# An mLSTM layer's sigmoids placed behind all its exponentials, and longer planned landings for small transfers

## The chip, the cores and the metric

The kernel runs on one core of one Trainium2 chip. The metric is the device time of one execution in microseconds (us), the median of several runs. A core has a matrix engine (TensorE, PE in the profile; PEld is its weight load), a vector engine (VectorE, DVE), a scalar engine (ScalarE, ACT), a general engine (GpSimd, POOL) and a queue for transfers (SyncE, SP). Each engine works through its own list of instructions in order; the engines wait for each other by semaphores alone.

## The reference, cut to what matters

A trunk of two layers over 256 tokens of width 1024, in float32. Each layer is a half-step SwiGLU, a mixer and another SwiGLU, each followed by a layer norm of the scaled sum. The mixer of the first layer is a bidirectional mLSTM, that of the second a windowed attention. Cut to the lines the change touches:

```python
p = x @ w_in                               # q, k, v, the output gate o, and gates i, f of both directions
wts = jnp.exp(dmat - m_out[..., None])     # per head and direction, from the scanned gates
s_qk = jnp.einsum('bhcjd,bhcsd->bhcjs', q, k) * wts
num = jnp.einsum('bhcjs,bhcsv->bhcjv', s_qk, v) + ...
h = num / den[..., None]
h = (h - mu) * lax.rsqrt(var + LN_EPS)     # per head
out = jax.nn.sigmoid(o.astype(jnp.float32)) * h
return out.astype(x.dtype) @ w_out
```

So an mLSTM layer has two nonlinear functions on ACT after its gates: exponentials for the weights of four heads, and sigmoids for the output gate.

## The kernel before, in words

Every product is made in three passes over a high and a low part of both operands (`mm3`): ACT writes the high part (`w_hi`, `k_hi`, `a_hi`), DVE the rest (`w_lo`, `k_lo`, `a_lo`). The SwiGLU stages and the value projection use a seven-product scheme; POOL adds some of its weight sums by accumulating transfers.

In the mixer, `qk` (units named `q`) projects queries and keys of two heads at a time. The last unit of a pair evacuates `kT` and calls `weights(h)`: POOL broadcasts the row maxima `most` over the partitions (`partition_broadcast`), ACT makes six exponentials into `wt` from `ucol`, POOL masks the diagonal blocks (`affine_select`). `scores(h)` (H0 to H3) multiplies keys by queries on PE, then by `wt` on DVE, and splits into `a_hi` and `a_lo`. `mixed(h)` (M0 to M3) multiplies by the values, divides by `den` and normalises; POOL raises `hrs` to the power -0.5, and the next DVE steps wait for that. `gate_units` (units `u`) make the output gate on PE. The first half of it for both token blocks is done early and only copied to `sg`; `sigmoids` (named `sig`) later loads the sigmoid's table and turns these copies into sigmoids. `gate_out` multiplies `h` by `sg`.

`MIXES` lists these pieces in the order in which the program is recorded; it sets PE's order outright. The order on ACT, DVE, POOL and SP is worked out by a planner (`Book`). It gives each step a due time, counted back from its readers, and then places steps one after the other by readiness and due time, with a cost for each. Of a transfer from POOL it assumes that it lands `LANDING + LOADING` (3600 ns) after its issue, and in the due times likewise. These costs order the work; they do not run on the chip.

A table load (`preload_act_table`) is ordered behind the users of the table before it, and each exponential or sigmoid behind the load recorded last. In the order before, the sigmoid's load stands ahead of the exponentials of heads 2 and 3, and three of the loads among these, and one further on, are in no line of the kernel: the compiler puts a load where a function's table isn't the one last loaded.

The small tensors that POOL loads are `few` (gate weights, gate biases, norm gain, attention sinks; each its own transfer) and `most`.

Of the kernel before, what the change touches and what calls it, by code (L numbers as in the profile page):

```python
# [50 lines left out]
OWN = [(5, 0), (6, 0), (7, 0)]  # L51
MIXES = ('P1*2 u*4 P2*2 u*2 p u*2 x1 u*4 x3 g x2 u*4 x4 S1*2 S2*2 S4*2 S3*2 q*7 A22*2 q*1 c q*29 '
         'sig q*1 H0 q*2 H1 q*8 M0 q*16 u*2 H2 M1 u*1 H3 u*3 M2 u*2 M3 u*8')
FIRST = "P1*2 d T1 P2*2 S1*2 S2*2 d S3*2 S4*2 d A22*2 T0"
FULL = "P1*2 d T1 P2*2 S1*2 S2*2 d S3*2 S4*2 d A22*2 T0 d"
SHUT = "P1*2 d T1 P2*2 S1*2 S2*2 d*2 S3*2 S4*2 A22*2 T0"
# [3 lines left out]
ISSUE = 600.0  # L60
LANDING = 2200.0
LOADING = 1400.0
ADDING = 5500.0
QUEUED = 6000.0
RING = {"SP": (2000.0, 1250.0), "POOL": (2900.0, 1150.0)}
# [182 lines left out]
SILU, EXPS, SIGMOID = "silu", "exps", "sigmoid"  # L248
TABLE = {AF.Silu: SILU, AF.Exp: EXPS, AF.Ln: EXPS, AF.Sigmoid: SIGMOID}


class Book:
# [13 lines left out]
    def note(self, engine, name, args, kw):  # L266
        views = [x for x in [*args, *kw.values()] if isinstance(x, View)]
        outs = [args[0]] if args and isinstance(args[0], View) else []
        if "accum_out" in kw:
            outs.append(kw["accum_out"])  # L270
        if name == "tensor_tensor_reduce":
            outs.append(args[-1])
        ins = [v for v in views if not any(v is o for o in outs)]
        s = Step(len(self.steps), engine, name, args, kw, outs, ins)
        self.steps.append(s)
        for v in views:
            if v.room not in s.rooms:
                s.rooms.append(v.room)
        for r in s.rooms:
            if r.kind == "const":  # L280
                continue
            if r.first is None:
                r.onto = r.kind == "bank" and engine != "PE"
                r.first, r.nth = s.n, len(self.rooms[r.kind])
                self.rooms[r.kind].append(r)
            r.last = s.n
            r.left += 1
            r.steps.append(s)
        for v in ins:
            r, (q, i) = v.room, v.place()  # L290
            for p in q:
                s.deps.update(r.writer[p, i].tolist())
        for v in outs:
            r, (q, i) = v.room, v.place()
            inside = np.zeros(r.n, bool)
            inside[i] = True
            for p in q:
                s.deps.update(r.writer[p, i].tolist())
                s.deps.update(r.pe[p, i].tolist())
            kept = []  # L300
            for other, q_, i_ in r.readers:
                if other is s:
                    continue
                if set(q_) & set(q) and inside[i_].any():
                    s.deps.add(other.n)
                    if set(q_) <= set(q) and inside[i_].all():
                        continue
                kept.append((other, q_, i_))
            r.readers = kept
            for p in q:  # L310
                r.writer[p, i] = s.n
                r.pe[p, i] = -1
        for v in ins:
            r, (q, i) = v.room, v.place()
            if engine == "PE":
                for p in q:
                    r.pe[p, i] = s.n
            else:
                r.readers.append((s, q, i))
        if name.startswith("preload"):  # L320
            s.deps.update(self.table_users)
            self.loaded, self.table_users = s.n, [s.n]
        elif name == "activation" and args[2] in TABLE:
            s.deps.add(self.loaded)
            self.table_users.append(s.n)
        s.deps -= {-1, s.n}
        self.cost(s)
        return s
# [64 lines left out]
    def latest(self):  # L393
        steps = self.steps
        extra = [[] for _ in steps]
        for kind, rooms in self.rooms.items():
            held, free = [], HOMES[kind][1]
            for r in rooms:
                if free:
                    free -= 1  # L400
                else:
                    held.sort(key=lambda x: x.last)
                    old = held.pop(0)
                    assert old.last < r.first, ("no room", kind, r.name, [x.name for x in held])
                    for s in old.steps:
                        extra[s.n].append(r.first)
                held.append(r)
        t = 0.0
        for s in steps:
            if s.engine == "PE":  # L410
                s.due = t
                t += s.takes
        for s in reversed(steps):
            if s.engine == "PE":
                continue
            after = s.later + s.takes
            if s.name == "dma_start":
                after += ADDING + LANDING if s.kw.get("accum_op") is not None else LANDING + LOADING
            s.due = min([steps[d].due for d in [*s.succ, *extra[s.n]]], default=t + 5000.0) - after

    def sequence(self):
# [54 lines left out]
        while len(given) < len(steps):  # L476
            best = None
            for e, list_ in todo.items():
# [7 lines left out]
                for n in cands:  # L486
                    s = steps[n]
# [21 lines left out]
            s = steps[n]  # L509
# [7 lines left out]
            s.lands = s.end + s.later  # L517
            if s.name == "dma_start":
                if e == "POOL" and s.kw.get("accum_op") is None:
                    s.lands = s.end + LANDING + LOADING  # L520
                elif loads < len(RAMP):
                    dma = s.lands = RAMP[loads]
                    rings.t = dma - RING[e][1]
                    loads += 1
                else:
                    for n_, t_ in rings.add(s).items():
                        steps[n_].lands = t_ + SPARE[steps[n_].engine]
                        if steps[n_].engine == "SP":
                            dma = max(dma, t_) if n_ == n else dma
                    loads += 1  # L530
# [1097 lines left out]
```

## Time and profile before

| | |
|---|---|
| median of 3 runs | 916.67 us (916.41 to 917.3) |
| profiled execution | 916.12 us, span 914.4 us |
| busy: PE, DVE, ACT, POOL | 98%, 90%, 72%, 18% of the span |
| moved by DMA | 220.07 MB, mean 241 GB/s |
| table loads on ACT | 10, 12.8 us in all |

The span is from the first instruction to the last; the execution's time is 1.7 us longer. In timeline rows the columns are start and length in us, engine, line, operation, output and inputs by the program's names, shapes and count; brackets hold the idle time ahead of it and what ended it. "Issue" there means that nothing the profile shows was waited for. All recorded operations share one line of the source, so they are told apart by their tiles.

### The profile page before, as it was taken

The page shows a single profiled execution, that of the slowest core. Times are in us where ns is not written, and L with a number is a line of the kernel's source. Part 1 is how long each engine was busy: PE and PEld are TensorE (multiplying, and loading weights), DVE is VectorE, ACT ScalarE, POOL GpSimd, SP SyncE. Part 2 cuts the span into 40 slices and gives each one's busy share as a digit, 9 for nine tenths or more (in the row PEclk, how much of TensorE's full clock was granted, in tenths as well). Part 3 has the DMA queues.
Part 4 walks back from the last instruction along what each step waited for, and adds up shares of the span by engine and source line. Part 5 has one row for each costly group of instructions (what it writes and reads, how often), then busy time and mean ns, then how long its engine had stood idle before and what let it go on. Part 6 is the DMA issues. An engine that isn't in the chain of part 4 may idle for free.

```text
span 914.4 us, 12652 instructions
## 1 busy us (share of the span) xinstructions
PE 893.3 (98%) x4375; PEld 744.0 (81%) x4375; DVE 825.4 (90%) x1011; ACT 659.7 (72%) x927; POOL 163.6 (18%) x200
## 2 busy tenths in 40 slices
PE   9999999999879999999999999999999999999996
PEld 7888888888867888888888888888898788888785
DVE  7999998799677999999889999997789999999974
ACT  6777676686856887776768867776689888677651
POOL 0121221220311211121011211130132231112100
PEclk9999999999999999999999999999999999999999
DMA  9999998937367889999985899999532778999931
GB/s 317 379 306 268 272 322 263 285 78 228 121 211 223 212 229 324 259 279 310 322 254 131 233 316 299 263 265 365 197 117 80 213 173 232 319 262 275 293 88 46
DMA packets 107744, 220.07 MB, mean 241 GB/s; under 512 B 7288, under 2 KB 23696, under 8 KB 107680
## 3 DMA queue, kind: packets, MB, share of 16 engines
q1 hardware_dynamic: 84000, 174.09, 53.9%
q0 software_dynamic: 23680, 45.18, 28.7%
q8 instruction: 34, 0.56, 0.2%
q14 instruction: 30, 0.25, 0.1%
HBM read 218.18 MB, written 1.05 MB: 240 GB/s over the span
## 4 chain that ended last, share of the span: by engine, by line
PE 71%; DVE 14%; issue 7%; ACT 4%; DMA 3%; POOL 1%; DVEq 0%; POOLq 0%; ACTq 0%
PE pw L597 44%; PE py L597 26%; DVE w_lo L597 7%; DMA b<-in_ffn_w_in_dram 2%; DVE b L597 1%; DMA raw<-in_ffn_w_out_dram 1%; ACT sc L597 1%; DVE e L597 1%; ACT L597 1%; ACT wt L597 1%; ACT w_hi L597 1%; DVE x L597 1%; DVE pr L597 0%; DVE h L597 0%; DVE pv L597 0%
## 5 line engine op out<-in xcount | busy, mean ns | idle before, releaser
L597 ACT CAST w_hi<-b 128x1024 fp32r<-128x1024 f32 x280 | 291.8, 1053 | 104.4 <-PE py L597 48.3
L597 DVE TENSOR_TENSOR w_lo<-b,w_hi 128x1024 fp32r<-128x1024 f32 x280 | 334.4, 1219 | 10.5 <-ACT w_hi L597 10.0
L597 PE MATMUL pw<-w_hi,S 128*128 128x512 f32 x640 | 205.8, 391 | 0.2 <-DVE h_lo L597 0.2
L597 DVE TENSOR_TENSOR w_lo<-raw,w_hi 128x1024 fp32r<-128x1024 f32 (+1 forms) x150 | 178.8, 1208 | 10.9 <-ACT w_hi L597 9.9
L597 POOL DMA_DIRECT2D b<-in_ffn_w_in_dram x80 | 96.9, 1214 | 502.8 <-DVE b L597 201.4
L597 ACT CAST w_hi<-raw 128x1024 fp32r<-128x1024 f32 (+1 forms) x150 | 155.1, 1041 | 36.0 <-PE pw L597 15.6
L597 PE MATMUL pw<-w_hi,xT_hi 128*128 128x512 f32 (+1 forms) x400 | 157.2, 395 | 1.4 <-DVE h_lo L597 1.0
L597 PE MATMUL pw<-w_hi,xT_lo 128*128 128x512 f32 (+1 forms) x400 | 154.8, 389 | 0.0
L597 PE MATMUL pw<-w_lo,xT_hi 128*128 128x512 f32 (+1 forms) x400 | 153.4, 386 | 0.0
L597 PEld LDWEIGHTS pw<-w_hi,S 128*128 128x128 f32 x640 | 120.1, 188 | 26.6 <-DVE h_lo L597 1.6
L597 PE MATMUL py<-w_hi,h_hi 128*128 128x512 f32 x317 | 125.5, 396 | 0.0
L597 PE MATMUL pw<-w_lo,S 128*128 128x512 f32 x320 | 124.5, 389 | 0.0
L597 PE MATMUL py<-w_hi,h_lo 128*128 128x512 f32 x317 | 123.7, 390 | 0.0
L597 PE MATMUL py<-w_lo,h_hi 128*128 128x512 f32 x317 | 123.4, 389 | 0.0
L597 DVE TENSOR_TENSOR b<-b,b 128x1024 f32<-128x1024 f32 x74 | 90.2, 1221 | 0.8
L597 PEld LDWEIGHTS pw<-w_hi,xT_lo 128*128 128x128 f32 x400 | 75.3, 188 | 17.5 <-DVE xT_lo L597 2.1
L597 PEld LDWEIGHTS pw<-w_hi,xT_hi 128*128 128x128 f32 x400 | 75.3, 189 | 17.2 <-DVE h_lo L597 1.8
L597 PEld LDWEIGHTS pw<-w_lo,xT_hi 128*128 128x128 f32 x400 | 75.1, 188 | 13.9
L597 PEld LDWEIGHTS pw<-w_lo,S 128*128 128x128 f32 x320 | 60.1, 188 | 12.2
L597 PEld LDWEIGHTS py<-w_hi,h_lo 128*128 128x128 f32 x317 | 59.5, 188 | 12.7
L597 PEld LDWEIGHTS py<-w_lo,h_hi 128*128 128x128 f32 x317 | 59.6, 188 | 11.8
L597 PEld LDWEIGHTS py<-w_hi,h_hi 128*128 128x128 f32 x317 | 59.5, 188 | 11.6
(208 smaller groups left out, 1134.7 us busy)
## 6 DMA issues: line engine op xcount, KB each, us to landing
b<-in_ffn_w_in_dram SPq DMA_DIRECT2D x152, 512.0 KB, 8.1
raw<-in_ffn_w_out_dram SPq DMA_DIRECT2D x88, 512.0 KB, 8.3
b<-in_ffn_w_in_dram POOLq DMA_DIRECT2D x80, 512.0 KB, 9.0
raw<-in_ffn_w_in_dram SPq DMA_DIRECT2D x36, 256.0 KB, 6.2
raw<-in_ml_w_in_dram SPq DMA_DIRECT2D x16, 512.0 KB, 6.5
raw<-in_at_w_in_dram SPq DMA_DIRECT2D x12, 512.0 KB, 9.0
b<-in_ml_w_in_dram SPq DMA_DIRECT2D x8, 512.0 KB, 6.7
raw<-in_ml_w_out_dram SPq DMA_DIRECT2D x8, 512.0 KB, 3.8
```

The costliest lines, as they stand in the source:

```text
L597: getattr(engines[s.engine], s.name)(*[real(x) for x in s.args], **{k: real(x) for k, x in s.kw.items()})
```

## The change

In `MIXES` the piece `sig` moves from ahead of H0 to behind the last `q` unit, that is, behind the exponentials of all four heads. The planner now notes which table is loaded and asserts that each function finds its own. And for plain transfers by POOL it assumes 6600 ns to land into `most` and 9500 ns into `few`, in the due times and in the placing.

```diff
-         'sig q*1 H0 q*2 H1 q*8 M0 q*16 u*2 H2 M1 u*1 H3 u*3 M2 u*2 M3 u*8')
+         'q*1 H0 q*2 H1 q*8 M0 q*16 sig u*2 H2 M1 u*1 H3 u*3 M2 u*2 M3 u*8')
...
+FEW = {"most": 6600.0, "few": 9500.0}
...
+            self.table = EXPS if name == "preload_act_table_set" else TABLE[args[0]]
         elif name == "activation" and args[2] in TABLE:
+            assert self.table == TABLE[args[2]], args[2]
...
-                after += ADDING + LANDING if s.kw.get("accum_op") is not None else LANDING + LOADING
+                after += ADDING + LANDING if s.kw.get("accum_op") is not None else FEW[s.outs[0].room.name] if s.engine == "POOL" else LANDING + LOADING
...
-                    s.lands = s.end + LANDING + LOADING
+                    s.lands = s.end + FEW[s.outs[0].room.name]
```

The order on PE and on SP stays the same, instruction by instruction. On the other engines it differs at a few places; three matter to the prediction. (The new file is three lines longer, so its rows read L600 where the old ones read L597.)

The first is ACT where the first pair's keys are evacuated (`k_hi`), ahead of H0. Before:

```order
L597 CAST q_hi<-pw 128x512
L597 ACTIVATE wt<-wt,ucol 128x128 x9
L597 CAST v_hi<-e_1978 128x2x256
L597 CAST w_hi<-raw 128x1024
L597 ACTIVATE k_hi<-pw 128x512
L597 ACTIVATE w_hi<-raw,few 128x1024 x2
L597 ACTIVATE wt<-wt,ucol 128x128 x3
L597 CAST a_hi<-wt 128x768
L597 ACT_TABLE_LOAD x2
L597 ACTIVATE wt<-wt,ucol 128x128 x6
```

And now:

```order
L600 CAST q_hi<-pw 128x512
L600 CAST v_hi<-e_1978 128x2x256
L600 CAST w_hi<-raw 128x1024
L600 ACTIVATE w_hi<-raw,few 128x1024
L600 ACTIVATE wt<-wt,ucol 128x128
L600 ACTIVATE k_hi<-pw 128x512
L600 ACTIVATE wt<-wt,ucol 128x128 x11
L600 ACTIVATE w_hi<-raw,few 128x1024
L600 CAST a_hi<-wt 128x768
L600 ACTIVATE wt<-wt,ucol 128x128 x6
```

`k_hi` has moved from behind nine exponentials and two casts to behind one exponential, and two loads of a table are gone. DVE at the same place, from the first `k_lo` to the first `a_lo`, before:

```order
L597 SCALAR_TENSOR_TENSOR k_lo<-pw,k_hi 128x512
L597 TENSOR_TENSOR w_lo<-raw,w_hi 128x1024
L597 TENSOR_TENSOR wt<-pw,wt 128x2x256
L597 TENSOR_TENSOR wt<-pw,wt 128x2x128
L597 TENSOR_TENSOR w_lo<-raw,w_hi 128x1024
L597 TENSOR_TENSOR a_lo<-wt,a_hi 128x768
```

And now:

```order
L600 SCALAR_TENSOR_TENSOR k_lo<-pw,k_hi 128x512
L600 TENSOR_TENSOR w_lo<-raw,w_hi 128x1024 x2
L600 TENSOR_TENSOR wt<-pw,wt 128x2x128
L600 TENSOR_TENSOR v_lo<-e_1978,v_hi 128x2x256
L600 TENSOR_TENSOR wt<-pw,wt 128x2x128
L600 TENSOR_TENSOR wt<-pw,wt 128x2x256
L600 TENSOR_TENSOR v_lo<-e_1949,v_hi 128x2x256
L600 TENSOR_TENSOR a_lo<-wt,a_hi 128x768
```

The products by `wt` stand behind one more weight difference and a `v_lo`, and a product of head 1 has come between those of head 0.

The second place is ACT from the first M0 to the second pair's `k_hi`, ahead of H2 (`den` and `h` belong to the mixes). Before:

```order
L597 ACTIVATE w_hi<-raw,few 128x1024
L597 CAST a_hi<-wt 128x768
L597 ACTIVATE den<-py 128x1
L597 ACTIVATE w_hi<-raw,few 128x1024
L597 ACTIVATE sg<-sg 128x512
L597 ACT_TABLE_LOAD
L597 ACTIVATE wt<-wt,ucol 128x128 x3
L597 ACTIVATE h_2419<-py,den 128x256
L597 ACTIVATE h_2425<-py,den 128x256
L597 ACTIVATE wt<-wt,ucol 128x128 x3
L597 ACTIVATE k_hi<-pw 128x512
```

And now:

```order
L600 ACTIVATE w_hi<-raw,few 128x1024
L600 CAST a_hi<-wt 128x768
L600 ACTIVATE h_2388<-py,den 128x256
L600 ACTIVATE h_2394<-py,den 128x256
L600 ACTIVATE w_hi<-raw,few 128x1024
L600 ACTIVATE wt<-wt,ucol 128x128
L600 ACTIVATE k_hi<-pw 128x512
L600 ACTIVATE wt<-wt,ucol 128x128 x5
L600 ACT_TABLE_LOAD
L600 ACTIVATE den<-py 128x1 x2
```

The sigmoids of the copies (`sg<-sg`) and the loads around them no longer stand ahead of `k_hi`; one load of the sigmoid's table follows the last exponential. Over the program ACT has six table loads where it had ten.

The third place is POOL in the same stage. The rows `ISA wt<-most` are the broadcasts, a bare `ISA` is a change of POOL's code. Before:

```order
L597 DMA most<-scan 4x256 x2
L597 ISA
L597 ISA wt<-most 128x256 x3
L597 AFFINE_SELECT wt<-wt 128x256 x2
L597 ISA wt<-most 128x256 x3
L597 AFFINE_SELECT wt<-wt 128x256 x4
L597 ISA wt<-most 128x256 x2
L597 AFFINE_SELECT wt<-wt 128x256 x2
L597 ISA
L597 TENSOR_TENSOR hrs<-hrs,few 128x2 x4
```

And now:

```order
L600 DMA most<-scan 4x256 x2
L600 ISA
L600 ISA wt<-most 128x256 x4
L600 AFFINE_SELECT wt<-wt 128x256 x2
L600 ISA wt<-most 128x256 x2
L600 AFFINE_SELECT wt<-wt 128x256 x4
L600 ISA wt<-most 128x256 x2
L600 ISA
L600 TENSOR_TENSOR hrs<-hrs,few 128x2
L600 AFFINE_SELECT wt<-wt 128x256 x2
L600 TENSOR_TENSOR hrs<-hrs,few 128x2 x3
```

The second change of code now stands right behind the last broadcast, and the masks of head 3 stand behind it and behind the first `hrs`. Further up, POOL issues the loads of the gate biases and gate weights one or two places earlier among its accumulating loads; the norm gain comes ahead of one `rs`, and the attention sinks ahead of one accumulating load.

## The prediction, made before the change was run

> **What bounds the kernel now.** I read the page first (span and busy time), then the waits of TensorE (PE), then the timeline of the one stage where PE waits.
>
> ```profile
> span 914.4 us, 12652 instructions
> PE 893.3 (98%) x4375; PEld 744.0 (81%) x4375; DVE 825.4 (90%) x1011; ACT 659.7 (72%) x927; POOL 163.6 (18%) x200
> ```
>
> PE is idle for 914.4 - 893.3 = 21.1 us in all. Half of that lies in 50 us of the mLSTM mixer, which is where the change works. The busy time of each engine there, and in its first three pieces of 5 us (columns: stretch, length, PE, weight load, DVE, ACT, POOL, granted PE clock, DMA share, GB/s):
>
> ```profile
> 230.00:280.00 50.00, 39.62 (x255) 35.44 (x254) 37.45 (x76) 38.91 (x80) 12.17 (x20) 0.97 0.58 195
> 230.00:235.00 5.00, 2.04 (x18) 1.83 (x16) 0.60 (x1) 3.94 (x11) 3.26 (x7) 1.00 0.30 105
> 235.00:240.00 5.00, 3.98 (x19) 3.78 (x20) 3.98 (x5) 4.78 (x9) 1.60 (x4) 0.66 0.01 3
> 240.00:245.00 5.00, 5.00 (x44) 5.00 (x43) 4.67 (x8) 4.98 (x12) 0.77 (x2) 1.00 0.58 206
> ```
>
> No engine fills the 50 us: PE works 39.6, DVE 37.5, ACT 38.9. They wait for each other in turn. What PE waits for between 225 and 284 us (us in total, times, longest):
>
> ```profile
> PE pw L597 <- ACT k_hi L597: 6.0, 2, 3.8
> PE py L597 <- ACT h L597: 1.6, 1, 1.6
> PE py L597 <- DVE h L597: 0.9, 1, 0.9
> PE py L597 <- DVE wt L597: 0.7, 1, 0.7
> PE py L597 <- DVE xT_lo L597: 0.6, 1, 0.6
> PE pw L597 <- DVE k_lo L597: 0.4, 2, 0.2
> ```
>
> These add up to 10.2 us. A further loss is the granted clock of 0.66 after the longest wait: from 235 to 240 us 19 matmuls take 3.98 us, while from 240 to 245 us 44 take 5.00, 0.114 each; 19 at that pace are 2.2, so 1.8 are lost. I count 1.5, as the restart itself is in it. **Ceiling: 10.2 + 1.5 = 11.7 us.** PE's order is the same throughout, so the change can move time only through what PE waits for.
>
> **Part 1, the first k_hi.** PE has run out of work at 232.04 and waits for the evacuation `k_hi` of the first two heads:
>
> ```profile
> 231.76 0.28 PE L597 MATMUL pw<-xT_hi,w_lo 128*128 128x256 f32 x1
> 235.79 0.38 PE L597 MATMUL pw<-q_hi,k_hi 128*128 128x256 f32 x1 [3.75 <-ACT k_hi L597]
> ```
>
> ACT at that time, and until the second `k_hi`:
>
> ```profile
> 231.06 2.74 ACT L597 ACTIVATE wt<-wt,ucol 128x128 f32<-128x128 f32 x9 [6.31 <-POOL wt L597]
> 233.70 0.60 ACT L597 CAST v_hi<-e 128x512 fp32r<-128x512 f32 x1
> 234.21 1.04 ACT L597 CAST w_hi<-raw 128x1024 fp32r<-128x1024 f32 x1
> 235.16 0.58 ACT L597 ACTIVATE k_hi<-pw 128x512 fp32r<-128x512 f32 x1
> 238.90 0.83 ACT L597 CAST a_hi<-wt 128x768 fp32r<-128x768 f32 x1 [0.21 <-DVE wt L597]
> 239.75 2.57 ACT L597 ACT_TABLE_LOAD   x2
> 244.80 1.28 ACT L597 ACT_TABLE_LOAD   x1
> 250.19 1.28 ACT L597 ACT_TABLE_LOAD   x1
> 253.97 0.58 ACT L597 ACTIVATE k_hi<-pw 128x512 fp32r<-128x512 f32 x1
> ```
>
> Before, nine exponentials, `v_hi` and a weight cast stand ahead of `k_hi`. In the new order one exponential does. That one still waits for POOL's first broadcast until 231.06 (nine take 2.74, so about 0.29 each); `k_hi` then runs from 231.35 to 231.93, before PE runs out. The casts now stand where ACT idled 6.31 us. The wait of 3.75 goes and with it the slow clock: 3.75 + 1.5 = **5.25 us**. DVE's `k_lo` (0.69) still follows `k_hi`, so its 0.2 stays here.
>
> **Part 2, what is late next: the first mix M0.** M0 needs `a_hi` and `a_lo` of head 0. The DVE rows that price its new order:
>
> ```profile
> 235.77 0.69 DVE L597 SCALAR_TENSOR_TENSOR k_lo<-pw,k_hi 128x512 fp32r<-128x512 f32 x1 [5.17 <-ACT k_hi L597]
> 236.38 1.22 DVE L597 TENSOR_TENSOR w_lo<-raw,w_hi 128x1024 fp32r<-128x1024 f32 x1
> 240.16 0.95 DVE L597 TENSOR_TENSOR a_lo<-wt,a_hi 128x768 fp32r<-128x768 f32 x1
> 241.03 0.41 DVE L597 TENSOR_TENSOR wt<-pw,wt 128x256 f32<-128x256 f32 x1
> 241.37 1.28 DVE L597 TENSOR_TENSOR v_lo<-e,v_hi 128x512 fp32r<-128x512 f32 x2
> 243.71 0.68 DVE L597 TENSOR_TENSOR wt<-pw,wt 128x512 f32<-128x512 f32 x1
> ```
>
> From the new `k_lo` end, 232.65: two `w_lo` 2.4, small product 0.35, `v_lo` 0.6, small product 0.35, large product 0.65 (each a little under its row, since neighbours overlap) give 237.0; ACT's `a_hi` 0.83 gives 237.85, `a_lo` 0.95 gives 238.8. PE comes from 232.04 with 42 matmuls (two scores of 6, ten projection units of 3) at 0.12 plus the 0.2, so at 237.3. It waits 0.55, and before the third product, which needs `a_lo`, 0.7 more. **Minus 1.25 us**; before, both operands were ready. Bounds: 0.3 if DVE runs its two weight differences during PE's own wait, 1.5 if one takes longer.
>
> **Part 3, the second k_hi.** ACT's time from 231.06 to 254.55 has almost no idle: 23.5 us of work stand ahead of and in the second `k_hi`. Out of that go four table loads, each of this price:
>
> ```profile
> L597 ACT ACT_TABLE_LOAD x10 | 12.8, 1283 | 0.9 <-PEq L1615 0.8
> ```
>
> 4 x 1.28 = 5.1; of ten loads six stay. The two sigmoids (1.2), `v_hi` and the weight cast (1.4 with overlap) and five exponentials (1.4) also leave this stretch. 23.5 - 9.1 = 14.4, plus some 0.9 of waiting for `a_hi`'s input: ACT could be through `k_hi` at 246.4. PE, 7.9 us of work after M0's effective start at 238.6, delivers the input at about 246.5 and has 1.4 us of gate units after it. So PE, not ACT, comes last: the second wait (6.0 - 3.75 = 2.25) and its `k_lo` (0.2) go. **2.45 us.** Here the loads are worth something; ACT idles again after 257 us, so their 5.1 us are not themselves a gain.
>
> **Part 4, the waits of the tail** (ACT h, DVE wt, DVE h, DVE xT_lo: 3.9 with roundings). They come from one event on POOL:
>
> ```profile
> 246.75 1.86 POOL L597 PARTITION_BROADCAST wt<-most  x2 [2.01 <-issue]
> 254.14 0.41 POOL L597 TENSOR_SCALAR_AFFINE_SELECT wt<-wt 128x256 f32<-128x256 f32 x1 [1.12 <-ACT wt L597]
> 261.66 0.73 POOL L597 TENSOR_TENSOR hrs<-hrs,few 128x2 f32<-128x2 f32 x1 [7.12 <-issue]
> 262.43 0.74 DVE L597 TENSOR_SCALAR h<-h,hmv,hrs 128x256 f32<-128x256 f32 x2 [2.88 <-POOL hrs L597]
> ```
>
> After the last mask (254.55) POOL issues nothing for 7.1 us: the order has an ISA row there, a reload of POOL's code. DVE waits 2.88 for `hrs` behind it, and everything on DVE afterwards is late. Now the reload stands right behind the last broadcast. That broadcast follows DVE's first scaled `w_lo` of the output weight, which comes 2.4 us after `a_lo`: 241.2 + 1.86 + 7.1 = 250.2, `hrs` done 250.95, against 262.40 before. PE is only 6.7 us ahead there (5.25 - 1.25 + 2.45 = 6.45, and roundings), so DVE's wait shrinks to about 1.3. Head 3's masks, now behind `hrs`, end at 251.75; DVE wants them about 254. I leave 1.3 of the 3.9 standing (0.3 at ACT h, 1.0 at the final transposes): **2.6 us**. Bounds 0 and 3.9.
>
> The Trainium skill (GPSIMD Engine Reference, 2.1 Instruction dispatch) puts the first call of freshly loaded POOL code at about 6 us (5.95 measured), invisible in the profile. The row here says 7.12, and the reload decides part 4: by the page `hrs` would be ready 1.1 us earlier and the sum about 1.1 us better. I keep the row.
>
> **Part 5, the small transfers.** The planner now thinks they land later, and POOL issues them earlier: gate biases and gate weights ahead of an accumulating load, the norm gain ahead of `rs`, the sink row ahead of another accumulating load. Only the last is close:
>
> ```profile
> 600.37 1.20 POOL L597 DMA_DIRECT2D b<-in_ffn_w_in_dram  x1 [2.63 <-DVE b L597]
> 601.09 1.10 POOL L597 DMA_DIRECT2D few<-in_at_sink_dram  x1
> 610.71 0.79 POOL L597 TENSOR_SCALAR few<-few 128x16 f32<-128x16 f32 x1 [1.23 <-DMA few<-in_at_sink_dram]
> 611.17 2.00 ACT L597 CAST w_hi<-b 128x1024 fp32r<-128x1024 f32 x2
> ```
>
> POOL idled 2.63 us ahead of that load, so the sink's issue (1.10) fits in. The sink, queued behind the load, had landed when its reader started at 610.71, so I take the load to have landed by then too; the second of the two casts wants it at 612.1, and 1.4 us of delay would be hidden. Cost 0, bound 1.5; no gain, since PE nowhere waits for these tiles.
>
> **Sum:** 5.25 - 1.25 + 2.45 + 2.6 = 9.05 us. The profiled execution took 916.12 with a span of 914.4; the new span is 905.3. It lies 0.55 under the median of 916.67, which becomes **907.6 us**, 1.0% faster.
>
> **Rivals.** *Half of it stays.* DVE's 37.45 us of work in this stage get closer together; if its backlog keeps the tail's waits (part 4 worth 0) and the second `k_hi` keeps half of its wait, the gain is 5.25 - 1.25 + 1.2 = 5.2: 911.5 us. For it speaks that DVE idles hardly at all from `k_lo` on; against it, that the 2.88 wait has a cause of its own, which moves up.
> *The reload becomes the bound, and it is slower.* Head 3's masks, before ahead of the reload, now wait for it and for `hrs`. The point that decides: the last broadcast. If its buffer came free only where the reload began before (254.6), the masks would end at 263.2 and head 3's operands at about 266. PE would reach M3 at about 258.5, stand for some 7.5 us, and pay the slow clock (1.5) again: 9.05 - 9.0 leaves nothing, and the late tail behind it (1.6 + 0.9 again) makes it 919. Against it: the buffer follows DVE's `w_lo`, which moves up with everything. Each us that the broadcast comes later than 244 costs about one.
> *The change does not do what it says:* automatic loads return wherever an exponential meets a sigmoid's table. Then ACT's list keeps its length, but the first `k_hi` is ahead anyway. The order shows six loads, which excludes it; the small chance of no change is for a cancelling wait that I don't see (916.7).
>
> **How the numbers follow.** Forecast 0.72 (905 to 910), half 0.18, no change 0.04, slower 0.06. Range: from the ceiling, 916.67 - 11.7 = 905.0, to just past the half case, 912.0. A measurement of this kernel tells about 0.2%, 1.8 us; both first cases lie beyond it: faster 0.90, same 0.04, slower 0.06.
>
> **What would show it.** Right: `k_hi` starts within 0.5 us of the first exponential, no PE wait over 3 us and no clock under 1.00 between 230 and 270; six table loads; PE waits about 1 us for `a_hi` or `a_lo` before M0; the long POOL gap ahead of `hrs` starts some 11 us earlier. Wrong: PE waiting on `wt` or `a_hi` at M3 with POOL's masks late, a second clock drop, or a wait at 595 to 615 us on `b`.

## The result, and the profile after

The changed kernel takes **905.12 us** (median of 4 runs, 903.93 to 907.42) beside 916.98 us of the kernel before on the same chip (4 runs, 916.41 to 918.1): ratio **0.9872, 95% interval 0.985 to 0.9894**. Measured twice more beside the experiments it gave 0.9876 (0.9851 to 0.99; medians 905.16 and 915.21) and 0.988 (0.9848 to 0.9912; 906.02 and 916.13). The profiled execution took 904.78 us. The forecast was 907.6, the range 905.0 to 912.0.

The page of the changed kernel, its first row and its busy times:

```profile
span 903.0 us, 12647 instructions
...
PE 890.6 (99%) x4375; PEld 741.9 (82%) x4375; DVE 824.9 (91%) x1011; ACT 655.8 (73%) x923; POOL 168.4 (19%) x200
```

PE's idle time falls from 21.1 to 12.4 us; its busy time falls by 2.7 as well, 1.7 of which is the slow clock that is gone (3.4 us at half rate). The mixer, in the same pieces of time as before (stretch, length, PE, weight load, DVE, ACT, POOL, granted PE clock, DMA share, GB/s):

```profile
230.00:270.00 40.00, 38.28 (x254) 34.12 (x253) 37.89 (x78) 32.69 (x73) 14.46 (x20) 1.00 0.69 242
230.00:235.00 5.00, 4.78 (x39) 4.41 (x38) 3.63 (x6) 4.41 (x14) 4.54 (x6) 1.00 0.38 149
235.00:240.00 5.00, 4.18 (x33) 3.77 (x32) 4.70 (x8) 4.08 (x12) 3.88 (x6) 1.00 0.41 124
```

From 230 to 235 us PE now works 4.78 us instead of 2.04, and the clock is 1.00 over all 40 us. What PE waits for in the mixer (225 to 285 us; us in total, times, longest):

```profile
PE py L600 <- DVE a_lo L600: 0.7, 1, 0.7
PE pw L600 <- DVE k_lo L600: 0.4, 2, 0.2
PE py L600 <- DVE xT_lo L600: 0.4, 1, 0.4
PE py L600 <- ACT a_hi L600: 0.2, 1, 0.2
```

1.7 us stand where 10.2 stood. The rows of ACT, POOL and DVE behind that (start, length, engine, operation, count; in brackets the idle time ahead and what ended it):

```profile
230.59 0.40 ACT L600 ACTIVATE wt<-wt,ucol 128x128 f32<-128x128 f32 x1 [1.54 <-POOL wt L600]
230.90 0.58 ACT L600 ACTIVATE k_hi<-pw 128x512 fp32r<-128x512 f32 x1
...
241.42 0.96 POOL L600 PARTITION_BROADCAST wt<-most  x2 [1.24 <-DVE w_lo L600]
249.29 0.81 POOL L600 TENSOR_TENSOR hrs<-hrs,few 128x2 f32<-128x2 f32 x1 [6.91 <-DVE k_lo L600]
...
246.62 0.60 ACT L600 ACTIVATE k_hi<-pw 128x512 fp32r<-128x512 f32 x1
...
250.36 0.81 DVE L600 TENSOR_SCALAR h<-h,hmv,hrs 128x256 f32<-128x256 f32 x2
```

The first `k_hi` starts 0.31 us after the first exponential. POOL's reload gap starts at 242.38 (241.42 + 0.96) instead of 254.55, so `hrs` is there at 250.1 and DVE's next row has no wait in brackets (2.88 before). The bracket of that gap names `k_lo`, which was done at 248.31, 1 us before the gap ended; in another profile of the change the same gap is 7.14 us with nothing waited for. So I take it for the reload. Grouped, the table loads:

```profile
L600 ACT ACT_TABLE_LOAD x6 | 7.7, 1283 | 0.9 <-PEq L1618 0.8
```

PE's order is the same in both kernels, so the start of its n-th matmul can be compared directly. Start after less start before, in us, worked out from both traces:

```
matmul     us before   after less before
1080       240.1       -0.65    (-0.63 of it within the first 40 matmuls)
1120       250.9       -5.89    first k_hi passed
1160       255.7       -4.55    first products of M0 passed
1240       269.2       -7.13    second k_hi passed
1360       296.0       -10.81   end of the mixer
2840       619.4       -10.82
2880       628.8       -11.31
last       917.4       -11.54
```

(These clocks start 10.7 us ahead of the profile's, 10.5 after the change; the difference of 0.18 is in all rows.) The mixer gives 10.16 us. Without that 0.18, the offset of the first 40 matmuls lies between -0.9 and +0.9 in the profiles of all kernels here; that is chance.

### The profile page after: what moved, and what is told of

Read it like the earlier page. It is cut to its first block, busy times and chain, and to the rows that moved or that the text cites. A ratio compares the mean times of both kernels' runs of the same rounds, so it can differ in the third digit from the quotient of the medians.

```text
span 903.0 us, 12647 instructions
## 1 busy us (share of the span) xinstructions
PE 890.6 (99%) x4375; PEld 741.9 (82%) x4375; DVE 824.9 (91%) x1011; ACT 655.8 (73%) x923; POOL 168.4 (19%) x200
## 4 chain that ended last, share of the span: by engine, by line
PE 72%; DVE 15%; issue 6%; DMA 4%; ACT 2%; POOL 1%; DVEq 0%; POOLq 0%; ACTq 0%
PE pw L600 44%; PE py L600 28%; DVE w_lo L600 8%; DMA b<-in_ffn_w_in_dram 3%; DVE b L600 1%; ACT sc L600 1%; DVE e L600 1%; DMA raw<-in_ffn_w_in_dram 1%; DVE S L600 1%; DVE scan L600 1%; DVE x L600 1%; DVE pr L600 1%; DVE pv L600 0%; DVE xT_lo L600 0%; DVE sc L600 0%
## 5 line engine op out<-in xcount | busy, mean ns | idle before, releaser
L600 ACT CAST w_hi<-b 128x1024 fp32r<-128x1024 f32 x280 | 292.0, 1053 | 103.1 <-PE py L600 50.6
L600 DVE TENSOR_TENSOR w_lo<-b,w_hi 128x1024 fp32r<-128x1024 f32 x280 | 334.0, 1217 | 9.5 <-ACT w_hi L600 9.1
L600 PE MATMUL pw<-w_hi,S 128*128 128x512 f32 x640 | 205.7, 390 | 0.0
L600 POOL DMA_DIRECT2D b<-in_ffn_w_in_dram x80 | 97.1, 1217 | 501.0 <-DVE b L600 172.6
L600 DVE TENSOR_TENSOR w_lo<-raw,w_hi 128x1024 fp32r<-128x1024 f32 (+1 forms) x150 | 178.6, 1207 | 11.4 <-ACT w_hi L600 10.5
L600 ACT CAST w_hi<-raw 128x1024 fp32r<-128x1024 f32 (+1 forms) x150 | 155.1, 1041 | 37.1 <-PE pw L600 15.9
L600 PE MATMUL pw<-w_hi,xT_hi 128*128 128x512 f32 (+1 forms) x400 | 156.6, 393 | 1.4 <-DVE h_lo L600 0.8
L600 PE MATMUL pw<-w_hi,xT_lo 128*128 128x512 f32 (+1 forms) x400 | 154.5, 388 | 0.2 <-DVE xT_lo L600 0.2
L600 PE MATMUL pw<-w_lo,xT_hi 128*128 128x512 f32 (+1 forms) x400 | 153.3, 386 | 0.0
L600 PEld LDWEIGHTS pw<-w_hi,S 128*128 128x128 f32 x640 | 120.1, 188 | 26.1 <-DVE h_lo L600 1.1
L600 PE MATMUL py<-w_hi,h_hi 128*128 128x512 f32 x317 | 125.5, 396 | 0.0
L600 PE MATMUL pw<-w_lo,S 128*128 128x512 f32 x320 | 124.5, 389 | 0.0
L600 PE MATMUL py<-w_hi,h_lo 128*128 128x512 f32 x317 | 123.7, 390 | 0.0
L600 PE MATMUL py<-w_lo,h_hi 128*128 128x512 f32 x317 | 123.4, 389 | 0.0
L600 DVE TENSOR_TENSOR b<-b,b 128x1024 f32<-128x1024 f32 x74 | 90.1, 1218 | 0.9
L600 PEld LDWEIGHTS pw<-w_hi,xT_lo 128*128 128x128 f32 x400 | 75.1, 188 | 17.5 <-DVE xT_lo L600 2.2
L600 PEld LDWEIGHTS pw<-w_hi,xT_hi 128*128 128x128 f32 x400 | 75.0, 188 | 17.0 <-DVE h_lo L600 1.6
L600 PEld LDWEIGHTS pw<-w_lo,xT_hi 128*128 128x128 f32 x400 | 75.1, 188 | 13.9
L600 PEld LDWEIGHTS pw<-w_lo,S 128*128 128x128 f32 x320 | 60.1, 188 | 12.3
L600 PEld LDWEIGHTS py<-w_hi,h_lo 128*128 128x128 f32 x317 | 59.5, 188 | 12.7
L600 PEld LDWEIGHTS py<-w_lo,h_hi 128*128 128x128 f32 x317 | 59.6, 188 | 11.8
L600 PEld LDWEIGHTS py<-w_hi,h_hi 128*128 128x128 f32 x317 | 59.5, 188 | 11.6
```

Source lines behind the costliest of these rows:

```text
L600: getattr(engines[s.engine], s.name)(*[real(x) for x in s.args], **{k: real(x) for k, x in s.kw.items()})
```

## The experiments

All run beside the kernel before on the same chip, in three groups (1 to 4, 5 to 7, 8 to 10), each on a chip of its own; between groups the ratios are what can be compared. "In the mixer" is the difference of matmul starts from 1080 to 1360, as in the table above, in one profiled execution each. The question: the change has two parts, the sigmoids' place and the landing times. Which part moves which instruction?

**1. The sigmoids alone.** The change with the old landing times:

```diff
-FEW = {"most": 6600.0, "few": 9500.0}
+FEW = {"most": LANDING + LOADING, "few": LANDING + LOADING}
```

> The sigmoids moved alone; every planned landing is the old 3600 ns. ACT has six table loads, but the first k_hi stands behind nine exponentials and two casts, as before the change, and POOL's order around the masks is the old one. Theory 1 (the first wait hangs on the place of k_hi, and that place comes from the planned landing of most, not from the sigmoids): PE's first wait of 3.75 us and the slow clock stay; the second wait for k_hi (2.25) goes, and since head 3's exponentials and masks end about 5 us earlier, the reload and hrs do too, so some 2 us of the tail go: about 4 us, 913 us. Theory 2 (the part 1 to 4 gains all come with the sigmoids, the transfers are worth nothing, as the prediction's part 5 has it): all of the gain, 905 to 907 us.

Measured: 916.49 us, 0.9999 to 1.0023 of before: nothing. Both expectations missed. ACT's order still has nine exponentials, `v_hi` and a weight cast ahead of the first `k_hi`, and PE's longest wait in the mixer is that of before (the two longest):

```profile
PE pw L600 <- ACT k_hi L600: 3.8, 1, 3.8
PE py L600 <- DVE a_lo L600: 1.6, 1, 1.6
```

So moving the sigmoids takes four table loads away and the second `k_hi` wait with them, but not the first wait. In the mixer 1.3 us are gained. Two losses eat the rest. One is the clock: it is exactly half from 234.2 to 241.1 us, and a second time from 261.5 to 265.0 (rows in the last section). The kernel before, whose wait is of the same 3.75 us, has it from 236.4 to 239.8 alone. PE worked 9.4 us at half rate here and 3.3 before. Half of the difference, 3.1 us, is my estimate of what that costs; without it the mixer would have gained about 4.4, near the 4 of theory 1. The other loss, 2.4 us, is far away, at 639 us in the time of the table; experiments 6 and 8 explain it.

**2. The landing times alone.** The kernel before with `FEW` in the planner, `sig` in its old place:

```diff
+FEW = {"most": 6600.0, "few": 9500.0}
...
-         'q*1 H0 q*2 H1 q*8 M0 q*16 sig u*2 H2 M1 u*1 H3 u*3 M2 u*2 M3 u*8')
+         'sig q*1 H0 q*2 H1 q*8 M0 q*16 u*2 H2 M1 u*1 H3 u*3 M2 u*2 M3 u*8')
```

> The planned landings changed alone (6600 and 9500 ns); the sigmoids stay ahead of the exponentials of heads 2 and 3, so ten table loads stay. The first k_hi stands behind one exponential, and the reload right behind the last broadcast. Theory 1: the first wait and the slow clock go (5.25 us), M0 waits about 1 to 2 us since a load and a sigmoid stand ahead of a_hi, the second k_hi is late by about 2.6 us (four loads and two sigmoids, 6.3 us, against some 2.3 us that ACT idles after the change), and most of the tail's waits go: about 6 us, 911 us. Theory 2 (transfers worth nothing): 916.5 to 917 us.

Measured: 910.68 us, ratio 0.9946 (0.9928 to 0.9964); 5.2 us in the mixer. The expectation from the forecast's parts held, the one that gave the transfers nothing fell. The first `k_hi` is behind one exponential here, and POOL's order is that of the change. What is left is the second `k_hi`, PE's longest wait, behind two of the loads:

```profile
PE pw L599 <- ACT k_hi L599: 3.1, 1, 3.1
```

```profile
245.65 1.28 ACT L599 ACT_TABLE_LOAD   x1
...
248.63 1.28 ACT L599 ACT_TABLE_LOAD   x1
249.92 0.40 ACT L599 ACTIVATE wt<-wt,ucol 128x128 f32<-128x128 f32 x1
250.23 0.58 ACT L599 ACTIVATE k_hi<-pw 128x512 fp32r<-128x512 f32 x1
```

The wait brings 3.4 us at half clock with it (250.9 to 254.3), which the shorter wait at this place in the kernel before (2.25) did not.

So the place of the first `k_hi`, the largest term of the forecast, comes from the planned landing, not from the sigmoids. Alone the parts are worth nothing that can be measured, and 0.5%; together 1.3%.

**3. The first `k_hi` put back.** The change, with that one step's due time later, which puts it behind nine exponentials:

```diff
+        held = [s for s in steps if s.engine == "ACT" and s.outs and s.outs[0].room.name == "k_hi"]
+        for s in held[:1]:
+            s.due += 30000.0
```

> The changed kernel with the first k_hi alone put behind nine exponentials, by a later due time; six loads, and the reload still ahead of one mask of head 3 and of hrs. If the prediction's part 1 is right in size, a wait of PE returns of nine exponentials less one (2.3 us), less what PE still has to do: about 2 us, without a clock drop since it is shorter than the 3.75 us that had one; M0's wait of 0.8 goes in exchange, so 1.2 to 2 us slower than the change, 906.5 to 907.5 us. If the place of k_hi is worth its whole 5.25 us by itself: 910 us. If other cover takes its place: 905 us.

Measured: 912.87 us, ratio 0.9966 (0.9954 to 0.9979). Against the change that is 0.94% by the ratios, 8.6 us (7.7 by the times), more than any expectation. PE waits 4.6 us for `k_hi`, and the clock is half for 6.8 us; after that the planner had placed the reload later as well (`hrs` at 257.23). About 2 us of the wait are not the edit's place of `k_hi`: POOL's first broadcast took 5.09 us in this trace, 2.8 to 3.6 in all others, and why is not shown. ACT's rows there:

```profile
227.78 1.16 ACT L603 ACTIVATE w_hi<-raw,few 128x1024 fp32r<-128x1024 f32 x1
232.75 2.74 ACT L603 ACTIVATE wt<-wt,ucol 128x128 f32<-128x128 f32 x9 [3.82 <-POOL wt L603]
235.40 0.57 ACT L603 ACTIVATE k_hi<-pw 128x512 fp32r<-128x512 f32 x1
```

The row is on the path, and its price is not the wait alone.

**4. The reload put back.** The change, with the last two masks of head 3 ahead of the first `hrs`, and so ahead of POOL's reload:

```diff
+        masks = [s.n for s in steps if s.name == "affine_select"][-2:]
+        first = next(s for s in steps if s.engine == "POOL" and s.outs and s.outs[0].room.name == "hrs")
+        for n in masks:
+            first.deps.add(n)
+            steps[n].succ.append(first.n)
```

> The changed kernel with both masks of head 3 ahead of POOL's reload, as before the change; ACT's order is the changed one but for one row. The reload can then start only after the last exponential (about 249 us) and hrs comes at about 256 in place of 249.3. Theory 1 (the tail's waits came from the reload by way of DVE's wait for hrs): DVE waits 3 to 5 us for hrs again and PE waits 2 to 3.5 us at M2, M3 or the transposes: 907 to 909 us. Rival (the tail's waits came from DVE's backlog after the late k_hi): no PE wait comes back, 905 us.

Measured: 908.86 us, ratio 0.9918 (0.9889 to 0.9946). The median is within the expectation, but two executions took 906.9 and two 910.8, and the trace is of one of the longer ones. In it the first `k_hi` keeps its early place, `hrs` is late again by 8 us, and 4.1 of the change's 10.2 us in the mixer are gone: 2.4 of it as waits of PE, and 1.6 as a half clock (261.9 to 265.3) that neither the change nor the kernel before has there.

```profile
257.31 0.73 POOL L605 TENSOR_TENSOR hrs<-hrs,few 128x2 f32<-128x2 f32 x1 [7.20 <-issue]
```

The waits of the tail do come from the reload, as part 4 has it. Whether its place is worth more than the 2.6 us given there is not settled: by their ratio to the kernel before, the two shorter executions lie only 2 to 3 us above the change.

**5. Two table loads put back.** The change, with loads of the exponentials' table recorded ahead of the exponentials of head 2 (three lines, two of which end up as rows of their own):

```diff
+                if h == 2 and d == 0:
+                    for _ in range(3):
+                        nc.scalar.preload_act_table_set("natural_log_exp_and_others")
```

> The change with two more loads of the exponentials' table on ACT, right ahead of the exponentials of head 2, that is between a_hi of head 0 and the second k_hi; eight loads instead of six, all other orders unchanged. They put 2 x 1.28 = 2.6 us on ACT. Theory (ACT has slack there: it idles 0.85, 0.43 and 0.92 us before the second k_hi, and PE has 1.4 us of other work at hand): 0 to 0.5 us slower than the change, 905.1 to 905.7. Rival (a table load costs its time on the path): 2.6 us slower, 907.7.

Measured: 906.93 us, ratio 0.9902 (0.987 to 0.9934), beside 905.16 of the change: 1.8 us slower in the medians, with intervals that overlap, and 2.5 us in the mixer of the traces. The forecast's reading, 0 to 0.5, missed; the rival is nearer. But the run tells less than it was meant to: the planner answered the loads with other orders on ACT and DVE, not unchanged ones. DVE now makes a `w_lo` ahead of the first `a_lo`, and PE's longest wait is that:

```profile
PE py L600 <- DVE a_lo L600: 1.6, 1, 1.6
```

0.9 of the loss stands there, the rest in the tail. What two loads cost in an order that is otherwise the same stays open.

**6. Only `most`, and 7. only `few`.** The change with one of the two landing times:

```diff
-FEW = {"most": 6600.0, "few": 9500.0}
+FEW = {"most": 6600.0, "few": LANDING + LOADING}     # 6
+FEW = {"most": LANDING + LOADING, "few": 9500.0}     # 7
```

> The change, but of the two new landing times only that of `most` (6600 ns); `few` (gate weights, biases, norm gain, sink row) is planned with the old sum again. In the mixer the order of ACT, DVE, POOL and PE is then word for word that of the change; only the places where POOL issues the transfers of `few` are the old ones (the sink row behind the accumulating load again). Theory (the planned landing of `most` alone moves k_hi and the reload): 904.5 to 906.0, as the change. Rival (the earlier transfers of `few` carry half of what the landings were worth alone, 5 us): about 907.5 to 911.

> The change, but only `few` with its new landing time (9500 ns); `most` with the old sum. The mixer has then the order of the run with the sigmoids moved alone, the transfers of `few` stand as in the change. Theory (the landing of `few` is worth nothing): as with the sigmoids alone, 915.5 to 917.0. Rival (the transfers of `few` issued earlier take the change's 0.5 us at 600 us, or more): 913 to 915.

Measured: only `most` 908.25 us, 0.9912 (0.9885 to 0.9939); only `few` 914.34 us, 0.9978 (0.9963 to 0.9992); the change beside them 905.16. With `most` the mixer gains its full 10.1 us; with `few` it gains 2.0. So the planned landing of `most` sets the mixer's order. But both theories missed and both times lie in the rivals' ranges: the change is 3.1 us faster than `most` alone, and `few` alone is 0.33%, 3.0 us, faster than the sigmoids alone by the ratios. The trace with `most` alone loses 3.6 us at 639 us in the time of the table (matmuls 2926 to 2938). POOL there, and below it the cast on ACT that is late:

```profile
590.65 1.10 POOL L600 DMA_DIRECT2D few<-in_at_sink_dram  x1
...
599.91 1.14 POOL L600 TENSOR_SCALAR few<-few 128x16 f32<-128x16 f32 x1 [7.00 <-DMA few<-in_at_sink_dram]
601.02 1.24 POOL L600 DMA_DIRECT2D b<-in_ffn_w_in_dram  x1
...
610.76 1.05 ACT L600 CAST w_hi<-b 128x1024 fp32r<-128x1024 f32 x1 [4.51 <-DMA b<-in_ffn_w_in_dram]
```

The sink row takes 9.3 us from issue to its reader. The planner, which thinks 3.6, has put the reader ahead of an accumulating load of a weight; POOL stands for 7 us, the load goes out late, and the weight's cast waits 4.51 us. PE's own wait behind it is 1.8 us; 1.7 more go to a half clock that follows (621.0 to 624.5). The run with the sigmoids alone has the same rows (a wait of 7.10 for the sink), the same wait of PE without the half clock, and loses its 2.4 us there; `few` alone does not have them. The kernel before has its reader behind that load: it is only in the new order of the mixer that the old landing time puts it ahead.

**8. That one row moved.** Kernel 6, with the sink's reader behind the two loads; the orders of PE, ACT and DVE are unchanged:

```diff
+        sink = next(s for s in steps if s.engine == "POOL" and s.name == "tensor_scalar" and s.outs[0].room.name == "few")
+        load = [s for s in steps if s.name == "dma_start" and s.kw.get("accum_op") is not None][61]
+        sink.deps.add(load.n)
+        load.succ.append(sink.n)
```

> The change with only `most` with its new landing time (908.25), with one row moved on POOL: the instruction that reads the sink row stands behind the two accumulating loads that it held up, instead of ahead of the first. Nothing else moves. Theory (the 3 us that this kernel lost to the change come from that reader, which waits 7 us for its transfer with the load queued behind it): 904.5 to 906, as the change. Rival (they come from the other transfers of `few`, or from chance in the stage at 600 to 640 us): about 907.5 to 908.5.

Measured: 906.32 us, 0.9885 (0.9851 to 0.9918), beside 906.02 of the change, 0.3 above the theory's range. The theory holds: the load goes out 7.2 us after the sink's issue (10.4 in kernel 6), its wait is for DVE, and the loss is gone.

```profile
591.37 1.10 POOL L604 DMA_DIRECT2D few<-in_at_sink_dram  x1
...
598.55 1.22 POOL L604 DMA_DIRECT2D b<-in_ffn_w_in_dram  x1 [4.93 <-DVE w_lo L604]
...
602.70 0.81 POOL L604 TENSOR_SCALAR few<-few 128x16 f32<-128x16 f32 x1
```

**9. `few` alone, on the kernel before.** `sig` in its old place, `most` with the old sum, `few` with 9500:

```diff
+FEW = {"most": LANDING + LOADING, "few": 9500.0}
```

> The kernel before (sigmoids in their old place), with only `few` planned with its new landing time. The mixer keeps the order of before; on POOL the transfers of `few` go earlier. Theory (before has the reader of the sink row already behind the load, so there is nothing to win): within 0.2% of before. Rival (some executions of before lose 2 to 3 us at the sink row, and this mends them): 0.2 to 0.3% faster, and a narrower spread.

Measured: 915.53 us, 0.9979 to 1.0013 of before. Nothing to win there, as expected: before, the reader stands behind the load already. The longer landing of `few` only keeps the change from a loss that its other parts would bring.

**10. The first `k_hi` by hand.** Kernel 7 (sigmoids moved, `few` alone), with ACT's order mended by two added dependencies:

```diff
+        held = next(s for s in steps if s.engine == "ACT" and s.outs and s.outs[0].room.name == "k_hi")
+        exps = [s for s in steps if s.engine == "ACT" and s.name == "activation" and s.args[2] is AF.Exp and s.outs[0].room.name == "wt"]
+        mix = next(s for s in steps if s.engine == "ACT" and s.outs and s.outs[0].room.name == "a_hi")
+        for first, later in (held, exps[1:9]), (mix, exps[12:]):
+            for s in later:
+                s.deps.add(first.n)
+                first.succ.append(s.n)
```

> The kernel with the sigmoids moved and only `few` with its new landing time, and in it ACT's order mended by hand: of the nine exponentials that stood ahead of the first k_hi seven go behind it (two stay ahead), and a_hi of head 0 keeps its place ahead of the exponentials of heads 2 and 3. POOL keeps the old order: all six masks ahead of the reload, the reload ahead of hrs. Theory (the place of the first k_hi and the place of the reload are the two effects of the longer landing of `most`): the first is had, the second not, so about where the change with late reload stood (908.86), a little above since the second k_hi stands behind the last exponentials: 908.5 to 910.5. Rival (the longer landing works by something else): no better than without the edit, 913.5 to 915.

Measured: 913.04 us, 0.9966 (0.9946 to 0.9986): the theory's number missed, the rival's was nearer. The trace shows why. One exponential was left ahead of the casts, and ACT stands at it:

```profile
231.03 0.40 ACT L607 ACTIVATE wt<-wt,ucol 128x128 f32<-128x128 f32 x1 [6.31 <-POOL wt L607]
231.34 0.60 ACT L607 CAST v_hi<-e 128x512 fp32r<-128x512 f32 x1
231.85 1.04 ACT L607 CAST w_hi<-raw 128x1024 fp32r<-128x1024 f32 x1
232.79 1.14 ACT L607 ACTIVATE w_hi<-raw,few 128x1024 fp32r<-128x1024 f32 x1
233.84 0.38 ACT L607 ACTIVATE wt<-wt,ucol 128x128 f32<-128x128 f32 x1
234.13 0.57 ACT L607 ACTIVATE k_hi<-pw 128x512 fp32r<-128x512 f32 x1
```

Taking seven exponentials away brought `k_hi` only 1 us nearer, because three casts (2.5 us from the first start to the end of the last) queue behind the first exponential's 6.31 us wait for POOL. PE still waits 2.7 us, and that is enough for half a clock from 234.0 to 240.8.

So the longer landing of `most` does two things to ACT's order here, and the runs that lack one of them still wait. It puts the casts ahead of all exponentials (their 2.5 us are in the way in this run), and all exponentials but one behind `k_hi` (the other eight take 2.3 us in experiment 3, where the casts are ahead).

## Why the prediction was right, and where it was not

The time lies 2.5 us under the forecast and 0.1 above the lower end of the range. That end was the ceiling: all of the mixer's waits and the slow clock, 11.7 us. The mixer gave 10.2 of these, and the other two measurements beside the kernel before differ by 10.1 us in the medians. So some 1.7 us of the 11.9 here are not the mixer's, and that the time came so near to the end of the range, or stayed inside it, is in part chance. Step by step, by the table of matmul starts:

- **Part 1, first `k_hi`**: forecast 5.25, measured 5.24. The wait went and the slow clock with it (1.65 lost, since PE worked 3.30 us at half rate, against the 1.5 counted).
- **Part 2, M0 waits**: forecast -1.25, measured -1.34; 0.16 for `a_hi` and 0.66 for `a_lo` are wait rows, the rest is in none.
- **Part 3, second `k_hi`**: forecast 2.45, measured 2.58. `k_hi` starts at 246.62 (ACT through by 246.4 was forecast). That four loads and the sigmoids between them go is what does it, by the run that kept them (wait of 3.1). Its sentence that the 5.1 us of loads "are not themselves a gain" was not settled: the run with two loads put back lost 1.8 us, but in other orders.
- **Part 4, the tail**: forecast 2.6 with 1.3 left standing, measured 3.68. This is the term that was mis-sized. Of the 3.9 only the 0.4 at `xT_lo` stayed. `hrs` was done at 250.1, not 250.95, and DVE didn't wait for it at all where 1.3 were expected. The 1.3 did not follow from the prediction's own numbers: with `hrs` 11.45 us earlier and DVE 6.7, a wait of 2.88 is gone. The gap itself measured 6.91, near the 7.1 taken. The mechanism is shown by the run with the reload put back, its size only roughly.
- **Sum**: 9.05 forecast, 10.16 measured in the mixer. Some 0.7 after 600 us and 0.65 at the start are in no part. Neither is the change's, as far as the traces show: 0.3 to 0.5 of the first lie between matmuls 2840 and 2880, where every other trace here gains as much on this one of the kernel before.
- **Part 5, the small transfers, failed as a step.** It read them as transfers that PE doesn't wait for: "Cost 0 ... no gain". Their landing times are inputs of the planner, and that of `most` sets the place of the first `k_hi` and of POOL's reload, parts 1 and 4: without it the mixer gains 2.0 us (kernel 7), with it 10.2. The time came out right because parts 1 to 4 were worked out from the new order itself and not from the line of the diff that caused it. And the sink row, which it priced by what the transfer's issue does to the load behind it (bound 1.5), costs 2 to 4 us in the new order of the mixer where its reader stands ahead of a load; in the order before there was nothing to win.
- **Rivals.** The case in which half stays (911.5) did not come, though the landing times alone give nearly that (910.68), with part 3 missing. The reload did not become a bound: the last broadcast came at 241.42, well ahead of the 244 named. The automatic loads did not return: six are in the trace.
- **What would show it** was all seen: `k_hi` 0.31 us after the first exponential, no wait over 0.7 in the mixer, clock 1.00, six loads, about 0.8 us ahead of M0, the gap ahead of `hrs` 12 us earlier.

## What to carry to other kernels

Where a planner sets the order, a landing time or cost in it is a change of code: compare the orders first, and ask of each moved row what stands behind it on its engine. A wait at the head of an engine's list is best filled by putting ahead of it what doesn't depend on it; here three casts behind the first exponential held `k_hi` up by 2.5 us, about as much as eight exponentials (2.3). And two edits that each leave one wait of 3 us or more in the stage may give less alone than together, here nothing and 5 us against 10: price them together, with the clock.

## What was not expected of the hardware

**The clock goes by windows of 3.41 us.** In every trace here the granted clock is recorded as 1.00 or exactly 0.50, and the edges of these records lie whole multiples of 3.41 us apart (in the kernel before, 67 windows of full rate up to 236.40, then one of half). Cut along these edges, the work of PE in a window goes with the clock of the next. The kernel before, at its first wait for `k_hi` (columns as in the mixer's rows above):

```profile
232.99:236.40 3.41, 0.50 (x2) 0.30 (x2) 0.63 (x2) 3.41 (x7) 2.18 (x5) 1.00 0.00 0
236.40:239.82 3.42, 3.30 (x15) 3.30 (x16) 3.17 (x5) 3.19 (x7) 0.41 (x1) 0.50 0.02 5
```

The sigmoids alone, at the same wait and at the second drop:

```profile
230.82:234.23 3.41, 0.34 (x3) 0.14 (x2) 0.00 (x0) 3.41 (x10) 1.67 (x5) 1.00 0.18 72
234.23:237.65 3.42, 2.73 (x11) 2.51 (x12) 2.50 (x4) 3.42 (x7) 1.09 (x3) 0.50 0.02 5
237.65:241.06 3.41, 3.41 (x18) 3.41 (x17) 3.25 (x6) 2.68 (x8) 1.36 (x3) 0.50 0.17 41
258.13:261.54 3.41, 1.47 (x7) 0.94 (x5) 2.33 (x6) 0.38 (x2) 0.73 (x1) 1.00 0.41 167
261.54:264.95 3.41, 3.27 (x15) 3.27 (x16) 3.41 (x7) 1.59 (x6) 0.00 (x0) 0.50 0.68 191
```

The ten drops in these traces (leaving out the last 20 us of each) all follow a window in which PE worked 0.3 to 1.65 us. No drop follows one with 1.73 or more; one with 1.63, near the end of the kernel before, had none either. So the border lies near half a window. Half rate then lasted a second window where PE worked 1.8 to 2.7 us in the first (four times), and ended after one where it worked 3.2 or more (six times). Nothing between one and two windows was seen, and each cost up to 1.7 us.

So the length of a wait does not tell by itself. The 3.75 us of the kernel before and of the sigmoids alone brought one window and two, by what PE did behind the wait. The kernel before's second wait of 2.25 us is spread over two windows with 2.3 and 2.1 us of work and cost no clock. With the reload put back, waits of 0.9 and 1.6 us fell mostly into one window, left 1.13 us of work in it and brought a drop. The wait of 1.8 us behind the sink row left 1.65 us in one window with `most` alone, and the clock fell; with the sigmoids alone it left 2.5 us in each of two, and it did not. The edges lie at other places in each trace, so I take it, without a run that shows it, that one kernel can pay this in some executions and not in others.

The Trainium skill (TensorE: Matmul & The Clock Gate, Part 1: The HAM clock gate) speaks of a free-running window of about 3.4 us, and of half rate after an idle one. The traces agree with the window, 3.41 us here; but a window with 1.65 us of work, not an idle one, was enough for half rate.

**A small transfer's landing and what waits behind it.** The two transfers of `most` land in 1.7 us each:

```profile
DMA to landing us min/median/max: 1.7/1.7/1.7
```

Their reader, POOL's first broadcast, starts 6.8 us after the issue is through, behind a reload of POOL's code. The first two rows are the change's, the last the kernel before's:

```profile
219.62 1.21 POOL L600 DMA_DIRECT2D most<-scan  x2 [16.55 <-ACT w_hi L600]
227.59 4.21 POOL L600 PARTITION_BROADCAST wt<-most  x4 [6.76 <-ACT v_hi L600]
227.82 4.04 POOL L597 PARTITION_BROADCAST wt<-most  x3 [6.54 <-issue]
```

The bracket of the change's row names `v_hi`, which was done at 226.79, 0.8 us before; the kernel before has nearly the same gap with nothing waited for. So the 6600 ns that the planner now takes for a landing describe the reload. The sink row did take 9.3 us from its issue to its reader, whose wait its landing ended, so there 9500 ns describe the transfer. The reload ahead of `hrs` showed as a gap of 6.7 to 8.1 us in these runs.
